# A 4096-cubed matmul with gelu: the check reads A's first block later, and one summed unit of B is read from the input

## The chip, the cores and the metric

The kernel runs on one core of a Trainium2 chip. The metric is device time in microseconds (us), of which the median of the timed runs counts. The core has five instruction streams: TensorE (PE), VectorE (DVE), ScalarE (ACT), GpSimd (POOL) and SyncE (SP). In this kernel POOL only issues transfers into the core (and a few within DRAM), and SP only issues stores.

## The reference

```python
def reference(a, b):            # a: [4096, 4096] f32, b: [4096, 4096] f32
    x = np.matmul(a, b)
    return 0.5 * x * (1 + np.tanh(np.sqrt(2 / np.pi) * (x + 0.044715 * x**3)))
```

## The kernel before, in words

A and B are read as f32 and land as f16 (the transfer converts). The product is computed by a Strassen-like scheme with seven products P1 to P7 of half-size blocks: A and B each have quadrants "11", "12", "21", "22", and a product takes a sum of quadrants of A times a sum of quadrants of B. The output is cut into 16 groups (mb, nb): mb is one of four bands of rows, nb one of four bands of columns. A band's quadrant of B has two chunks along the inner dimension (`c` 0 and 1).

*Groups 0 to 3* ("raw groups", `first_group`, `raw_group`) are computed for mb = 0 while B is read for the first time. Sums of B's quadrants are made there on VectorE (`combine2`, L964) and stored in DRAM as summed units, one for each (nb, product name): `unit(nb, name)`, DRAM tile `k_unit`, four quarters of 512 KB, stored on SP by `store_unit`, fetched later on POOL by `fetch_unit_to`.

*The 12 other groups* run as six late pairs (`late_pair`, numbered 4, 6, 8, 10, 12, 14, about 170 us each, starting near 419, 590, 760, 931, 1101 and 1271 us). Pairs 4, 8 and 12 work on nb 3 and 0, pairs 6, 10 and 14 on nb 1 and 2. Each pair goes through the seven products (`both`), and for each obtains the two summed units of B by `whole_pair`. Some products need a plain quadrant of B and no sum: those named in `FROM_INPUT` are not stored by a raw group but read again from the input, as 16 pieces of 128 KB (8 for a chunk), until a pair named in `STORE_AT` has stored them:

```python
elif (nb, name) in FROM_INPUT and (nb, name) not in on_hand:
    ...
        dma("POOL", dst, src, [], toks, "raw_b", batch=("bl", nb, name, cc))
    ...
else:
    for q in (2 * cc, 2 * cc + 1):
        fetch_unit_to(nb, name, q, cells[q])
```

*The first group* (mb = 0, nb = 0) starts when nothing is in the core. It opens with chunk 0 of A11 times that of B12 (`first_steps`, which issue eight A loads and eight B loads of 128 KB ahead of all others), then `plain_pe` (L2260) takes plain quadrants, A11 times B11 first and, four products later, the one with B21 (each of 32 matmuls); then come the sums. `load_b_` and `load_a_` issue the loads: B's pieces are 128 KB, A's 256 KB. A arrives with its rows in the wrong dimension, so VectorE transposes each chunk (L656). Half-products (L744) follow, with sums of A and B from L964, and their results are copied on ScalarE (L1316, L2384) and added on VectorE (L1322).

*The check.* In f16 the result holds only for inputs of moderate size. The kernel therefore sums squares of A's rows and of B's columns (`stats["a"]`, `stats["b"]`), and a last test decides whether a general path has to run instead; in the runs here it does not. For A's first band ScalarE squares each 128x256 piece while it lies there (`weigh_row`, L684: an ACTIVATE with an accumulator, and the instruction that reads the accumulator). Later bands of A are squared in the pairs. For B the squares of nb = 0 are taken in the first group, by VectorE (L1405) or by ScalarE (L1408) as the table `SQ` says, and are added up on VectorE (L1413).

*Order.* All but the first steps is written down as operations with a number (class `Plan`), and a planner sorts them by costs and due times (`MOVE`, `WEIGHT`, `COST`). Its order is then corrected by tables of numbers: `EARLIER` moves an operation's due time, `AFTER` puts operation n behind m on its engine, `HOLD` makes one wait for another. PE's order is fixed. Each engine runs its stream in that order, so a POOL load that waits for its buffer holds the loads behind it. Names such as `bR_79`, `stage_87`, `aD_82` and `aT` are buffers in the core; a 128x2048 f16 cell is 512 KB, and a chunk is two cells.

Of the kernel before, what the change touches and what calls it, by code (L numbers as in the profile page):

```python
# [9 lines left out]
F16 = mybir.dt.float16  # L10
# [8 lines left out]
Q = 32  # L19
# [33 lines left out]
UNDER_WAY = {"POOL": [(0.68, 12.2)] * 4}  # L53
# [7 lines left out]
    "store": 1.345, "fetch": 1.38, "quarter": 1.6, "piece": 1.27, "out": 0.73, "raw_a": 1.3, "raw_b": 0.645,  # L61
    "raw_a0": 1.363, "raw_b0": 0.64, "tiny": 0.2, "out_half": 0.3,
}
WEIGHT = {
    "raw_a0": 1.31, "raw_b0": 1.06, "store": 2.0, "fetch": 2.42, "quarter": 2.16, "piece": 2.16, "raw_a": 1.11,
    "raw_b": 1.06, "out": 1.05,
# [15 lines left out]
def modes_of(**kw):  # L82
# [12 lines left out]
}  # L95
HOLD = {
   
}
AFTER = [
# [459 lines left out]
def half_path(  # L559
# [281 lines left out]
    def c(x):  # L841
        return ("c", x)
# [1681 lines left out]
```

## Time and profile before

| what | us |
|---|---|
| median of 3 runs | 1445.19 |
| fastest and slowest of them | 1443.98, 1448.59 |
| the profiled execution | 1448.0 |
| its span in the trace | 1446.4 |
| mean granted clock of PE | 0.999 |

The profile is of one execution. In rows of the trace the first number is the start in us from the span's start, the second the length; in brackets stands how long the engine was idle before it, and what released it. A row of the waits has the engine and line that waited, what it waited for, the sum in us, the count and the longest. A row of a window has the length, for each engine its busy time and instructions (PE, PEld, DVE, ACT, POOL), the granted clock of PE, the share of the transfer engines and GB/s. A row of the transfers has their count, size and the median us from issue to landing.

### The profile page before, as it was taken

The numbers are of one execution on the slowest core, as the hardware profiler recorded it, in microseconds if no ns is written. First come the engines' busy times: TensorE is split into PE (matmuls) and PEld (weight loads), VectorE is DVE, ScalarE is ACT, GpSimd is POOL, SyncE is SP. The second block draws the span as 40 slices with busy tenths as digits, with TensorE's granted clock in tenths as the row PEclk, the third lists the DMA queues.
The fourth block names the chain that finished last, engine by engine and source line by source line (L and its number), as shares of the span: only waits on it lengthen the run. The fifth ranks groups of instructions, "written<-read, shape, count | busy, mean of one in ns | idle before, by whom it ended". The sixth has DMA issues, their size and how long they took to land. (4 is left out here: it accounts for less than half of the span.)

```text
span 1446.4 us, 19351 instructions
## 1 busy us (share of the span) xinstructions
PE 1419.4 (98%) x6707; PEld 656.3 (45%) x6707; DVE 1238.0 (86%) x1331; ACT 692.1 (48%) x1492; POOL 487.5 (34%) x892
## 2 busy tenths in 40 slices
PE   8989999999999999999999999999999999999998
PEld 3434455465444444444444444444444444444443
DVE  2997797998889999979897988887998998878876
ACT  4966656358866313543655313353463622333133
POOL 6554245054225152324423342332322231231220
PEclk9999999999999999999999999999999999999999
DMA  9999999999999998989979897998998967796773
GB/s 171 203 241 272 311 298 266 338 237 271 295 299 248 335 201 231 310 276 276 321 259 318 274 216 270 257 248 276 280 348 241 302 160 228 273 313 217 260 256 140
DMA packets 207674, 380.99 MB, mean 263 GB/s; under 512 B 20944, under 2 KB 119760, under 8 KB 207568
## 3 DMA queue, kind: packets, MB, share of 16 engines
q0 software_dynamic: 150400, 247.52, 71.7%
q1 hardware_dynamic: 57168, 132.15, 24.4%
q8 instruction: 55, 0.90, 0.2%
q14 instruction: 51, 0.42, 0.1%
HBM read 339.74 MB, written 134.22 MB: 328 GB/s over the span
## 5 line engine op out<-in xcount | busy, mean ns | idle before, releaser
L1972 PE MATMUL acc<-bR 128*128 128x512 f16 x1568 | 346.8, 379 | 0.4 <-DVE bR L964 0.2
L1972 PEld LDWEIGHTS <-bR 128*128 128x128 f16 x1984 | 193.9, 98 | 235.0 <-DVE bR L964 1.3
L1972 PE MATMUL acc<-bR,aT 128*128 128x512 f16 x1280 | 283.4, 379 | 4.8 <-DVE bR L964 3.9
L1972 PEld LDWEIGHTS <-aT 128*128 128x128 f16 x1664 | 162.6, 98 | 202.0 <-issue 6.2
L838 POOL DMA_DIRECT2D bR<-k_unit x224 | 121.4, 545 | 367.9 <-PE acc L1972 265.2
L964 DVE TENSOR_TENSOR bR<-bR 128x4096 f16<-128x4096 f16 (+1 forms) x114 | 210.6, 1858 | 29.6 <-PE acc L1972 20.3
L838 POOL DMA_DIRECT2D bR<-in_b_dram x320 | 173.6, 546 | 159.0 <-DMA bR<-in_b_dram 61.3
L1984 ACT COPY acc<-acc 128x512 f32<-128x512 f32 x168 | 95.7, 574 | 274.7 <-PE acc L1972 247.4
L1322 DVE TENSOR_TENSOR y<-acc,y 128x512 f32<-128x512 f32 x269 | 177.1, 685 | 25.1 <-PE acc L1972 24.2
L1972 PE MATMUL acc<-bR,aD 128*128 128x512 f16 x736 | 163.6, 379 | 0.0
L1296 ACT ACTIVATE y<-y 128x512 f32<-128x512 f32 x174 | 105.3, 625 | 112.2 <-DVE y L1322 111.9
L1972 PEld LDWEIGHTS <-aD 128*128 128x128 f16 x1024 | 100.2, 98 | 120.8
L744 PE MATMUL acc<-bR,aT 128*128 128x512 f16 x544 | 119.9, 379 | 2.2 <-DVE y L1322 1.2
L744 PEld LDWEIGHTS <-aT 128*128 128x128 f16 x768 | 75.1, 98 | 92.3 <-issue 3.3
L1981 ACT COPY y<-acc 128x512 f32<-128x512 f32 x114 | 66.4, 585 | 94.5 <-PE acc L1972 87.1
L1408 ACT ACTIVATE y<-bR 128x1024 bf16<-128x1024 f16 x83 | 84.9, 1051 | 36.5 <-DVE y L1413 33.8
L838 POOL DMA_DIRECT2D stage<-in_b_dram x104 | 56.3, 546 | 121.9 <-PE acc L1045 32.3
L744 PEld LDWEIGHTS <-aD 128*128 128x128 f16 x608 | 59.4, 98 | 77.9 <-DVE aD L964 4.2
L1972 PE MATMUL acc<-stage,bR 128*128 128x512 f16 x416 | 94.0, 379 | 0.0
L1413 DVE TENSOR_TENSOR y<-y 128x1024 bf16<-128x1024 bf16 x102 | 70.0, 688 | 25.6 <-ACT y L1408 24.0
L1972 PE MATMUL acc<-stage,aT 128*128 128x512 f16 x384 | 86.8, 379 | 0.0
L1327 DVE TENSOR_TENSOR acc<-acc,y 128x512 f32<-128x512 f32 x115 | 78.9, 693 | 5.3 <-ACT y L1981 5.0
(128 smaller groups left out, 1769.0 us busy)
## 6 DMA issues: line engine op xcount, KB each, us to landing
bR<-k_unit POOLq DMA_DIRECT2D x224, 512.0 KB, 7.8
out_dram<-y SPq DMA_DIRECT2D x194, 256.0 KB, 6.8
bR<-in_b_dram POOLq DMA_DIRECT2D x328, 128.0 KB, 7.0
k_unit<-bR SPq DMA_DIRECT2D x78, 512.0 KB, 7.0
stage<-k_unit POOLq DMA_DIRECT2D x60, 512.0 KB, 7.0
bR<-in_a_dram POOLq DMA_DIRECT2D x64, 256.0 KB, 9.2
k_unit<-stage SPq DMA_DIRECT2D x30, 512.0 KB, 8.0
out_dram<-bR SPq DMA_DIRECT2D x56, 256.0 KB, 6.7
```

Of the source, the lines that this page charges most:

```text
L744: nc.tensor.matmul(acc, sa[:, j // 2, i * P : (i + 1) * P, j % 2], sb[:, j, :], start=start and j == 0, stop=stop and j == 3, skip_group_c ...
L838: return plan.add(queue, COST[queue], lambda: eng.dma_start(out=dst, in_=src), r=r, w=w, size=MOVE[what] * SPREAD, weight=weight, **kw)
L964: nc.vector.tensor_tensor(out=dst, in0=xa, in1=ya, op=ALU.add if op > 0 else ALU.subtract)
L1296: act("gelu", lambda: nc.scalar.activation(t, t, ACT.Gelu_apprx_tanh), [("f", f)], [("f", f)])
L1322: dve("add", lambda: nc.vector.tensor_tensor(out=sm(g), in0=bank(s, i), in1=sm(f), op=ALU.add), [("f", f)], [("f", g), ("p", s, i)])
L1327: dve("add", lambda: nc.vector.tensor_tensor(out=bank(s, i), in0=bank(s, i), in1=sm(f), op=ALU.add), [("f", f)], [("p", s, i)])
L1408: act("square", lambda t=t, src=src: nc.scalar.activation(t, src, ACT.Square), [c(cx)], [("f", f)], slack=60.0, lead=lead)
L1413: dve("add16", lambda t=t, u=u: nc.vector.tensor_tensor(out=u, in0=u, in1=t, op=ALU.add), [("f", f)], [("f", e)], slack=60.0, lead=lead)
L1972: nc.tensor.matmul(bank(w, i), sa[:, jx // 2, r * P : (r + 1) * P, jx % 2], bv[:, jx, :], start=p in "17" and jx == 0, stop=jx == NJ - 1, ...
L1981: act("copy", lambda: nc.scalar.copy(out=sm(f), in_=bank(w, i)), [("p", w, i)], [("f", f)])
L1984: act("copy", lambda: nc.scalar.copy(out=bank(*dst), in_=bank(*x)), [("p", *x)], [("p", *dst)])
```

## The change

1. *A's first band is squared later.* The 128 squares on ScalarE in the first group go, with the two small VectorE steps that added them up. In pairs 8 and 12 the four quadrants of that band are read again from the input: eight times a chunk (`new_chunk`), each by four POOL loads of 256 KB (32 in all), followed by eight ScalarE squares of 128x512 (64 in all); the chunk is then free again. `AGAIN` says before which product of the pair each one is placed.
2. *The unit (1, P1)* enters `FROM_INPUT`. Its raw group no longer stores it (four SP stores of 512 KB less there). Pairs 6, 10 and 14 take it from the input (48 POOL loads of 128 KB instead of 12 fetches of 512 KB). `STORE_AT` has 14 for it, so pair 14 stores it (four SP stores), after which nothing fetches it.
3. *Squares of B for nb = 0*: `SQ` is False throughout, so 12 squares of 128x1024 go from VectorE to ScalarE.
4. *Order.* B11's chunk 0 gets a lead of 500 over A21's, and the tables `MOVE`, `WEIGHT`, `EARLIER`, `HOLD` and `AFTER` are new.

PE's instructions are the same in number and order of work.

```diff
-SQ = {"12": True, "11": True, "22": False, "21": True}
+SQ = {'12': False, '11': False, '22': False, '21': False}
-FROM_INPUT = ((0, 'P1'), (0, 'P2'), (0, 'P3'), (1, 'P2'), (1, 'P3'), (3, 'P3'))
-STORE_AT = {(0, 'P1'): 4, (0, 'P2'): 4, (1, 'P2'): 14, (0, 'P3'): 8}
+FROM_INPUT = ((0, 'P1'), (0, 'P2'), (0, 'P3'), (1, 'P2'), (1, 'P3'), (3, 'P3'), (1, 'P1'))
+STORE_AT = {(0, 'P1'): 4, (0, 'P2'): 4, (1, 'P2'): 14, (0, 'P3'): 8, (1, 'P1'): 14}
+AGAIN = {8: {'P6': ('11', 0), 'P5': ('11', 1), 'P3': ('12', 0), 'P4': ('12', 1)}, 12: {'P6': ('21', 0), 'P5': ('21', 1), 'P3': ('22', 0), 'P4': ('22', 1)}}
+AGAIN_SLACK = 20.0
+LEAD11 = 500.0
-        load_b_("11", 0)
+        load_b_("11", 0, LEAD11)
...
-HOLD = {
-   
+    1268: 1267, 2046: 2154, 3152: 3249,
...
+    def weigh_again(quad, h, x0):
+        ih, kh = int(quad[0]) - 1, int(quad[1]) - 1
+        n = NX // 2
+        s, toks, t = chunk(x0).rearrange("p (x r) -> p x r", r=CH * RUN), [c(x0), c(x0 + 1)], rows_again[ih]
+        gate = [o for o in plan.ops if o.eng == "PE"][-CAST_BACK:][:1]
+        for g in range(4):
+            dma("POOL", s[g * Q : (g + 1) * Q, :, :], a_v[kh, g, :, ih * MH // Q + h * n : ih * MH // Q + (h + 1) * n, :],
+                [], toks, "raw_a", batch=("again", quad, h), slack=AGAIN_SLACK, after=gate)
+        for x in range(n):
+            r = h * n + x
+            act("weigh", lambda x=x, r=r: nc.scalar.activation(
+                s[:, x, :], s[:, x, :], ACT.Square, accum_out=t[:, kh, r : r + 1]),
+                [], [("again", ih), *toks], batch=("wa", quad, h), slack=SLACK)
+        if kh and h:
+            dve("small", lambda: nc.vector.tensor_reduce(
...
+            if name in again:
+                x = new_chunk()
+                weigh_again(*again.pop(name), x)
+                free_cells.extend((x, x + 1))
...
-            for r in range(NX):
-                act("weigh0", lambda r=r: weigh_first(quad, cc, (r,), next(junk)), toks,
-                    [("w0",), ("rows", 0), ("rows", 1)],
-                    batch=("w0", quad, cc), slack=FIRST_SLACK)
...
-        dve("stat", weigh_first_half, [("w0",)], [("sa", 0, 0), ("sa", 0, 1)], slack=300.0)
```

What moves on POOL, at three places. First the loads right behind the first steps: `bR_79` takes B11, chunk 0, and `stage_87` A21, chunk 0. Before:

```order
L838 DMA bR_79<-in_b_dram 32x4x512 x5
L838 DMA stage_87<-in_a_dram 32x16x256
L838 DMA bR_79<-in_b_dram 32x4x512 x3
L838 DMA stage_87<-in_a_dram 32x16x256
L838 DMA bR_75<-in_b_dram 32x4x512
```

After:

```order
L897 DMA bR_79<-in_b_dram 32x4x512 x8
L897 DMA stage_87<-in_a_dram 32x16x256 x4
L897 DMA bR_75<-in_b_dram 32x4x512
L897 DMA bR_80<-in_b_dram 32x4x512
L897 DMA bR_75<-in_b_dram 32x4x512
```

A21's loads now begin only when all eight pieces of B11 are issued.

Next, the loads up to the last piece of `bR_77`, which takes B21, chunk 0 (`bR_75`, `bR_74` and `bR_80` take other quadrants of B, `stage` and `aD` quadrants of A). The rows before follow directly on those of the place above; after, one row lies between (`stage_86`, two loads of A). Before:

```order
L838 DMA stage_86<-in_a_dram 32x16x256
L838 DMA stage_87<-in_a_dram 32x16x256 x2
L838 DMA stage_86<-in_a_dram 32x16x256 x2
L838 DMA bR_77<-in_b_dram 32x4x512 x2
L838 DMA stage_86<-in_a_dram 32x16x256
L838 DMA bR_77<-in_b_dram 32x4x512 x2
L838 DMA bR_75<-in_b_dram 32x4x512 x3
L838 DMA aD_82<-in_a_dram 32x16x256 x2
L838 DMA bR_75<-in_b_dram 32x4x512 x4
L838 DMA aD_82<-in_a_dram 32x16x256 x2
L838 DMA stage_87<-in_a_dram 32x16x256 x4
L838 DMA bR_77<-in_b_dram 32x4x512 x4
```

After:

```order
L897 DMA bR_75<-in_b_dram 32x4x512 x2
L897 DMA bR_74<-in_b_dram 32x4x512
L897 DMA stage_86<-in_a_dram 32x16x256 x2
L897 DMA bR_80<-in_b_dram 32x4x512
L897 DMA bR_74<-in_b_dram 32x4x512
L897 DMA bR_77<-in_b_dram 32x4x512
L897 DMA bR_75<-in_b_dram 32x4x512 x4
L897 DMA bR_80<-in_b_dram 32x4x512
L897 DMA bR_77<-in_b_dram 32x4x512 x6
L897 DMA bR_80<-in_b_dram 32x4x512
L897 DMA aD_82<-in_a_dram 32x16x256 x2
L897 DMA bR_77<-in_b_dram 32x4x512
```

Fewer pieces of A stand ahead of the last piece of `bR_77` now, and more of B.

Last, in pair 8, the loads of `stage_87` with eight raw pieces of B (chunk 1 of the unit for the next sum). Before:

```order
L838 DMA bR_77<-in_b_dram 32x4x512
L838 DMA bR_74<-in_b_dram 32x4x512
L838 DMA stage_86<-in_b_dram 32x4x512
L838 DMA bR_77<-in_b_dram 32x4x512 x5
L838 DMA bR_74<-in_b_dram 32x4x512 x3
L838 DMA stage_87<-in_b_dram 32x4x512 x8
L838 DMA bR_77<-in_b_dram 32x4x512
L838 DMA bR_75<-k_unit_233 128x2048
```

After:

```order
L897 DMA bR_74<-in_b_dram 32x4x512 x4
L897 DMA bR_73<-in_b_dram 32x4x512 x8
L897 DMA bR_74<-in_b_dram 32x4x512 x4
L897 DMA bR_75<-in_b_dram 32x4x512
L897 DMA bR_76<-in_a_dram 32x8x512
L897 DMA stage_87<-in_b_dram 32x4x512 x8
L897 DMA bR_76<-in_a_dram 32x8x512
L897 DMA bR_75<-in_b_dram 32x4x512 x7
L897 DMA bR_76<-in_a_dram 32x8x512
L897 DMA k_unit_240<-in_b_dram 32x4x512
L897 DMA bR_76<-in_a_dram 32x8x512
```

One of the four A loads of a second reading (`bR_76`) now stands directly ahead of the eight pieces of `stage_87`, the three others among those behind it.

More of the change, by code (lines that the diff above doesn't have):

```diff
@@ L1 @@
 from contextlib import ExitStack
-from itertools import cycle
 import concourse.bass as bass
@@ L52 @@
 BUSY = {"PE": 20.2, "DVE": 15.3, "ACT": 20.4, "POOL": 12.2, "SP": 5.0}
-UNDER_WAY = {"POOL": [(0.68, 12.2)] * 4}
+UNDER_WAY = {"POOL": [(0.68, 13.2)] * 4}
 LAG = 0.2
@@ L60 @@
 MOVE = {
-    "store": 1.345, "fetch": 1.38, "quarter": 1.6, "piece": 1.27, "out": 0.73, "raw_a": 1.3, "raw_b": 0.645,
-    "raw_a0": 1.363, "raw_b0": 0.64, "tiny": 0.2, "out_half": 0.3,
+    "store": 1.31, "fetch": 1.291, "quarter": 1.6, "piece": 1.27, "out": 0.743, "raw_a": 1.304, "raw_b": 0.649,
+    "raw_a0": 1.377, "raw_b0": 0.6444, "tiny": 0.2, "out_half": 0.3,
 }
 WEIGHT = {
-    "raw_a0": 1.31, "raw_b0": 1.06, "store": 2.0, "fetch": 2.42, "quarter": 2.16, "piece": 2.16, "raw_a": 1.11,
-    "raw_b": 1.06, "out": 1.05,
+    "raw_a0": 1.263, "raw_b0": 1.13, "store": 2.06, "fetch": 2.18, "quarter": 2.16, "piece": 2.16, "raw_a": 1.22,
+    "raw_b": 0.98, "out": 1.14,
 }
@@ L680, in load @@
             nc.gpsimd.dma_start(out=dst, in_=src)
-    def weigh_row(dst, src, to=None):
-        nc.scalar.activation(src if to is None else to, src, ACT.Square, accum_out=dst)
-    def weigh_first(quad, c, xs, to=None):
-        ih, kh = int(quad[0]) - 1, int(quad[1]) - 1
-        for x in xs:
-            k = ((kh * CH + c) * 2 + ih) * NX + x
-            weigh_row(stats["a"][:, k : k + 1], staged[quad, c][:, x, :], None if to is None else to[:, :])
-    def weigh_first_half():
-        t = tallies[:, 4 * NX : 6 * NX]
-        nc.vector.tensor_reduce(
-            out=t, in_=stats["a"].rearrange("p (k x) -> p x k", k=2 * CH), axis=AX.X, op=ALU.add
-        )
-        nc.vector.tensor_copy(out=stats["a"][:, : 2 * NX], in_=t)
     def gather(s):
@@ L792, in half_path @@
     before = {}
-    for n, whats in ((0, "A11_0a B12_0a A11_0b B12_0b T11_0a T11_0r T11_0s W11_0"),):
+    for n, whats in ((0, "A11_0a B12_0a A11_0b B12_0b T11_0a T11_0r T11_0s"),):
         for what in whats.split():
             half = what[-1] == "0" and what != "A11_0"
-            if what[0] == "W":
-                before.setdefault(n, []).append((weigh_first, (what[1:3], int(what[4]), range(NX))))
-                continue
             for h in (0, 1) if half else (None,):
@@ L1331, in half_path @@
     next_stage = [0]
-    rows = [tallies[:, 2 * ih * NX : 2 * (ih + 1) * NX].rearrange("p (k x) -> p k x", k=2) for ih in range(2)]
+    rows, rows_again = (
+        [tallies[:, 2 * k * NX : 2 * (k + 1) * NX].rearrange("p (k x) -> p k x", k=2) for k in (2 * n, 2 * n + 1)]
+        for n in range(2)
+    )
     seen_rows = set()
@@ L1369, in turn_quad @@
         seen_rows.add((mb, ih))
+    def weigh_again(quad, h, x0):
[13 more added lines that the diff above has]
+            dve("small", lambda: nc.vector.tensor_reduce(
+                out=stats["a"][:, ih * NX : (ih + 1) * NX], in_=t.rearrange("p k x -> p x k"), axis=AX.X, op=ALU.add,
+            ), [("again", ih)], [("sa", 0, ih)], slack=60.0)
     def load_raw(nb, quad, slot):
@@ L1432, in fn @@
                 )
-            dve("stat", fn, [("f", e), ("w0",)], [("f", f), ("sb", k)], slack=60.0)
+            dve("stat", fn, [("f", e)], [("f", f), ("sb", k)], slack=60.0)
     SB, SA, ST = (18, 19, 20, 21), (22, 23, 16, 17), (12, 13, 14, 15)
@@ L2058, in split_pair @@
                 then()
+        again = dict(AGAIN.get(ga, {}))
         def both(name, fresh, done):
+            if name in again:
+                x = new_chunk()
+                weigh_again(*again.pop(name), x)
+                free_cells.extend((x, x + 1))
             for what in CASTS.get((ga, name), ()):
@@ L2227, in first_group @@
         X, Y = 0, 1
-        junk = cycle((stats["b"].bitcast(F16), tallies.bitcast(F16)))
         S = {quad: slot_cells(b_slot[quad]) for quad in b_slot}
```

400 rows, old and new, of tables (AFTER, EARLIER) are left out of this document.

## The prediction

> **What bounds the kernel now.** I read the page's first part, then PE's waits, then PE's rows with idle time before them, then the DMA list of two stretches.
>
> ```profile
> PE 1419.4 (98%) x6707; PEld 656.3 (45%) x6707; DVE 1238.0 (86%) x1331; ACT 692.1 (48%) x1492; POOL 487.5 (34%) x892
> ```
>
> PE is busy 98% of 1446.4 us, so an edit that leaves the matmuls alone can only move PE's waits and its clock. The waits of the profiled execution, without the two of the start-up, are:
>
> ```profile
> PE acc L2260 <- DMA bR<-in_b_dram: 4.5, 3, 2.9
> PE acc L744 <- DVE aD L964: 4.4, 3, 1.9
> PE acc L1972 <- DVE bR L964: 4.1, 3, 2.4
> PE acc L744 <- DVE stage L964: 2.1, 2, 1.8
> PE acc L744 <- DVE y L1322: 1.2, 1, 1.2
> PE acc L744 <- ACT acc L2384: 1.0, 1, 1.0
> PE acc L1972 <- DMA bR<-in_b_dram: 0.8, 1, 0.8
> PE acc L1972 <- DMA bR<-k_unit: 0.2, 1, 0.2
> ```
>
> They sum to 18.3 us: the whole prize, beside the clock. Where they lie, by PE's rows (start, length, work, idle before it):
>
> ```profile
> 23.20 29.32 PE L2260 MATMUL acc<-bR,aT 128*128 128x512 f16 x128 [2.88 <-DMA bR<-in_b_dram]
> 53.15 0.38 PE L2260 MATMUL acc<-bR,aT 128*128 128x512 f16 x1 [0.63 <-DMA bR<-in_b_dram]
> 54.48 20.66 PE L2260 MATMUL acc<-bR,aT 128*128 128x512 f16 x95 [0.95 <-DMA bR<-in_b_dram]
> ...
> 94.38 3.63 PE L744 MATMUL acc<-bR,aD 128*128 128x512 f16 x16 [1.87 <-DVE aD L964]
> 115.70 7.07 PE L744 MATMUL acc<-aD,aT 128*128 128x512 f16 x32 [1.17 <-DVE aD L964]
> ...
> 180.32 7.07 PE L744 MATMUL acc<-stage,aD 128*128 128x512 f16 x32 [1.85 <-DVE stage L964]
> ...
> 448.55 3.61 PE L1972 MATMUL acc<-bR,aT 128*128 128x512 f16 x16 [1.48 <-DVE bR L964]
> 863.99 7.08 PE L1972 MATMUL acc<-bR,aT 128*128 128x512 f16 x32 [2.38 <-DVE bR L964]
> ```
>
> Three groups: the start to 116 us (4.5 + 4.4 + 1.0 = 9.9), the raw groups to 284 us (2.1 + 1.2 = 3.3), the late pairs (4.1 + 0.8 + 0.2 = 5.1). No row after 863.99 has an idle time: the last 577 us have nothing to win, only to lose.
>
> **The start: the order of the loads.** In the first 60 us POOL's loads run at the rate that the transfers allow.
>
> ```profile
> 23.20:26.61 3.41, 3.41 (x9) 1.26 (x9) 0.00 (x0) 0.00 (x0) 1.93 (x4) 0.54 1.41 197
> 26.61:30.02 3.41, 3.41 (x18) 1.57 (x16) 0.01 (x1) 0.03 (x1) 1.09 (x2) 1.00 1.45 196
> 31.49 0.54 POOL L838 DMA_DIRECT2D bR<-in_b_dram  x1 [0.77 <-DMA stage<-in_a_dram]
> 32.83 0.54 POOL L838 DMA_DIRECT2D bR<-in_b_dram  x1 [0.80 <-DMA stage<-in_a_dram]
> ```
>
> The windows' last column is GB/s: 196 to 197. POOL's issues stand 1.34 us apart there, waiting for A loads; an A load is 256 KB, 262 kB at 196 GB/s, 1.34 us too. So bytes ahead in the queue give the landing time.
>
> *B11, chunk 0.* Before, one A load lies within its last eight pieces, now none: it lands 1.34 us earlier, 2.88 becomes 1.54. *B21, chunk 0.* Counted in both orders up to its last piece, A has 8 of 128 KB and 16 of 256 KB before, 8 and 10 now; B has 32 and 38 pieces of 128 KB: 9216 KB before, 8448 KB now. 768 KB less is 786 kB, at 197 GB/s 4.0 us. It lands near 50.4 instead of 54.4, and PE, 1.34 us earlier, wants it at 51.2: 0.63 and 0.95 go. Together 2.9 us. Bounds 0 (another piece is late) and 4.5 (all three go).
>
> Then VectorE and ScalarE. ScalarE's rows to 130 us, VectorE's squares, POOL's hold, and the stretch 60 to 126:
>
> ```profile
> L684 ACT ACTIVATE stat_b<-stage 128x256 f16<-128x256 f16 x40 | 16.4, 409 | 9.1 <-DMA stage<-in_a_dram 9.1
> L684 ACT ACTIVATION_READ_ACCUMULATOR stat_b<-stage 128x1 f32 x40 | 7.7, 193 | 0.0
> L1408 ACT ACTIVATE bR<-bR 128x1024 bf16<-128x1024 f16 x9 | 9.2, 1048 | 7.9 <-DVE y L1413 5.2 <-DMA bR<-in_b_dram 2.7
> L1405 DVE TENSOR_TENSOR bR<-bR x9: 650/683/687, 32.9 to 71.8; 128x1024 bf16<-128x1024 f16 x9
> 88.32 4.28 POOL L838 DMA_DIRECT2D stage<-in_b_dram x8 [7.83 <-ACT tally L684]
> 60.00:126.00 66.00, 60.58 (x279) 26.98 (x277) 61.39 (x79) 43.89 (x144) 33.81 (x62) 1.00 1.21 242
> ```
>
> A row square costs ScalarE 0.409 + 0.193 = 0.60 us; 128 of them are 77 us, all before 116. They go, and 12 squares of B come from VectorE, 12 x 1.05 = 12.6 us: ScalarE has room, and POOL's hold of 7.83 us behind it goes. VectorE loses 12 x 0.68 = 8.2 us before 72 us. It is busy 61.39 of the 66 us in which PE waits 4.4 + 1.0 for its sums and for a ScalarE copy, so less backlog there shortens waits. But the second chunk of A21 is now loaded last of the first block: its transposes and sum come later, and I expect a new wait of 0.8 to 2 us near 81 us, where before has none. I take 5.4 down to 2.1: gain 3.3. Bounds: 5.4 (all go) and a loss of 0.5 (all stay, B21's gain merely waits elsewhere, plus a little). Start: 2.9 + 3.3 = 6.2 us, bounds -0.5 to 9.9.
>
> The clock after a wait, in three windows of one length:
>
> ```profile
> 863.99:867.40 3.41, 3.41 (x16) 1.56 (x16) 3.41 (x5) 1.08 (x2) 0.00 (x0) 1.00 0.97 359
> 94.38:97.80 3.42, 3.42 (x16) 1.58 (x17) 3.42 (x6) 0.00 (x0) 2.34 (x5) 1.00 1.22 198
> ```
>
> Behind the waits of 2.38 and 1.87 us the granted clock is 1.00; behind that of 2.88 it was 0.54 (23.20 to 26.61 above: 9 matmuls, 18 in the next window). That half cost 3.41 / 2 = 1.7 us. With a wait of 1.54 it may not come, but I count nothing: PE would reach B21 at 49.5 and wait there for 50.4, and the late sum of A21 stands behind it. By the Trainium skill, "TensorE: Matmul & The Clock Gate", section "What's actually happening", the half rate comes after a whole idle window of about 3.4 us; here 2.88 us sufficed, so the trace is stricter. By that rule a shorter wait would surely not halve the clock, and at most 0.8 us more would be left at B21.
>
> **The raw groups.** Four 512 KB stores of the unit (1, P1) go from SP's queue. 2.1 MB at the 303 GB/s below is 6.9 us of transfers. The wait at 180.32 is for a sum of late B pieces, which shared the wires with such stores; the whole stretch now starts earlier, so part of the room is eaten. I take a quarter of 3.3: 0.8. Bounds 3.3 and -1 (the B pieces also moved).
>
> **The pairs: what is added.** Rows of 126 to 283 us first, then of pair 8 (760 to 931 us):
>
> ```profile
> DMA packets 26391, 47.60 MB, mean 303 GB/s; under 512 B 2932, under 2 KB 15894, under 8 KB 26380
> bR<-in_b_dram POOLq DMA_DIRECT2D x82, 128.0 KB, 9.0
> stage<-in_b_dram POOLq DMA_DIRECT2D x16, 128.0 KB, 7.2
> ...
> DMA packets 22502, 44.62 MB, mean 261 GB/s; under 512 B 2284, under 2 KB 12268, under 8 KB 22490
> k_unit<-in_b_dram POOLq DMA_DIRECT2D x16, 128.0 KB, 7.3
> stage<-in_b_dram POOLq DMA_DIRECT2D x16, 128.0 KB, 6.6
> bR<-in_b_dram POOLq DMA_DIRECT2D x16, 128.0 KB, 5.3
> bR<-in_a_dram POOLq DMA_DIRECT2D x6, 256.0 KB, 11.7
> stage<-in_a_dram POOLq DMA_DIRECT2D x4, 256.0 KB, 8.3
> ```
>
> Pairs 8 and 12 each read 16 A pieces again (16 x 1.34 = 21 us of transfers, 16 issues) and square them: 32 squares, by width at most 1.05 + 0.19 us each, 40 us of a ScalarE that is 48% busy over a pair of 171 us. Hidden. A raw piece is read as f32 and lands as f16, so counts twice in memory: the raw groups carried 47.60 + 98 x 0.131 = 60.4 MB in 157 us, 385 GB/s, with 3.3 us of waits. Pair 8 carries 44.62 + 48 x 0.131 + 10 x 0.262 = 53.5 MB, and 8.4 more: 62 MB in 171 us, 362 GB/s. That is under what the raw groups bore. Pairs 6, 10 and 14 load (1, P1) as 16 raw pieces instead of four 512 KB units each: as many landed bytes, twice the reading, twelve issues more, on a POOL that is 34% busy. The words of the change say the unit is stored at its first reuse; its entry says 14, and the order has no fetch of it left: all three uses read the input.
>
> The order in pair 8 keeps the stall before 863.99:
>
> ```profile
> 826.95 0.56 POOL L838 DMA_DIRECT2D stage<-in_b_dram  x1 [15.35 <-DVE bR L964]
> 850.41 4.87 POOL L838 DMA_DIRECT2D stage<-in_b_dram  x8 [0.65 <-DMA bR<-in_b_dram]
> ```
>
> From the issue at 850.41 to PE at 863.99 are 13.6 us. Now, counted in PE's order, the buffer is freed 49 matmuls before its reader: 49 x 7.08/32 = 10.8 us, with an A piece just ahead. Stall 2.8 (1 to 5). Several other loads are released as close. I take the pairs' waits from 5.1 to 6.6: a loss of 1.5. Bounds: a gain of 5.1, and a loss of 7 (pairs 8 and 12 each lose what the raw groups lose, 3.5 us).
>
> **Sum.** -6.2 - 0.8 + 1.5 = -5.5 us. The profiled execution took 1448.0 us, 2.8 above the median 1445.2; 5.5 off the median is 1439.7.
>
> **Rivals.**
> *B, given back:* the gain is made by 126 us, but pairs 6 and 8 wait for it again: they run at the transfers' pace, and a PE that comes 6 us earlier finds loads released as late as before. For it: the pieces at 863.99 are 13.6 us in flight. Against it: loads there are released by PE and VectorE, which move along. Loss of 5 instead of 1.5: 1443.2.
> *C, slower:* each of the eight second readings holds a chunk and puts 4 x 1.34 = 5.4 us of transfers in front of the fetch behind it. Where a buffer is freed under 13.6 us before its reader, that adds to the stall. It decides once over 6.9 us are lost: two of eight such places at 5.4 are 10.8, so 1445.2 - 7.0 + 10.8 = 1449; three give 1454. Against: after 863.99 PE has no wait at all before, so pair 12 has slack to give.
> By the Trainium skill, "DMA: Bandwidth & Descriptors", section "Specifications", one core gets about 358 GB/s of memory; by it pair 8's 62 MB would need 173 us, 2 more than it has, and the sum would be 1441.7. The 385 GB/s of the raw groups is over that figure, so the trace speaks against it.
> *D, more:* the early waits nearly all go (9.9) and the pairs lose nothing: 1445.2 - 9.9 - 0.8 = 1434.5.
>
> **How the numbers follow.** My forecast 0.47 (its own range 1437 to 1442), B 0.25, C 0.15, D 0.13. The range reaches to D and to where C begins: 1434 to 1448. About 0.3% (4.3 us) is what a measurement of this kernel can tell from no change: faster is under 1440.9, slower over 1449.5. Faster 0.40 of mine and D: 0.53; same 0.07 and B: 0.32; slower 0.15.
>
> **What would show it.** In the profile after: the wait of 2.88 near 1.5 and no wait for B21; POOL no longer held by ScalarE; a new wait for A21's sum near 80 us; the matmul group at 115.70 starting near 109.5; no more than 7 us of waits after 419 us, one of them in pair 8 for a VectorE sum of stage pieces. I am wrong if group 115.70 starts after 113, or if a fetch behind a second reading of A stops PE.

## The result, and the profile after

| | before | after |
|---|---|---|
| median of the runs, us | 1445.03 (8 runs) | 1453.72 (8 runs, 1450.40 to 1461.48) |
| profiled execution, us | 1448.0 | 1451.07 |

The ratio is 1.0063, with a 95% interval of 1.0039 to 1.0086: slower by 8.7 us. The two profiled executions differ by 3.1 us only: that of before lies 3 us above its median, that of after 2.7 below its own. So the rows below show part of the loss, and single executions are read here only for waits that come back in several kernels. Of all executions reported in this document one, of the twelve of b_p1_not_stored, took 2521.79 us at a mean granted clock of 0.556; it is left out of that kernel's numbers.

PE's line of the page, then all that PE waited for in the execution after, down to 1.0 us (sum, count, longest):

```profile
PE 1421.8 (98%) x6707; PEld 656.0 (45%) x6707; DVE 1227.5 (85%) x1319; ACT 688.1 (47%) x1376; POOL 526.5 (36%) x960
```

```profile
PE acc L806 <- DVE aD L1023: 3.7, 1, 3.7
PE acc L2052 <- DMA bR<-in_b_dram: 2.7, 4, 1.5
PE acc L2052 <- DMA bR<-k_unit: 2.3, 3, 1.2
PE acc L2052 <- DVE bR L1023: 2.1, 2, 1.2
PE acc L806 <- DVE stage L1023: 1.5, 2, 1.1
PE acc L2052 <- ACT y L2061: 1.5, 2, 1.2
...
PE acc L2341 <- DMA bR<-in_b_dram: 1.4, 1, 1.4
PE acc L806 <- DMA stage<-in_b_dram: 1.3, 1, 1.3
...
PE acc L2052 <- ACT bR L1375: 1.0, 1, 1.0
```

Line 2052 is the matmul of the late pairs, 1972 before. Its waits are 9.6 us now (2.7 + 2.3 + 2.1 + 1.5 + 1.0), 5.1 before. PE's rows with idle time, from the start and from the pairs:

```profile
21.95 6.85 PE L2341 MATMUL acc<-bR,aT 128*128 128x512 f16 x31 [1.39 <-DMA bR<-in_b_dram]
...
82.31 8.67 PE L806 MATMUL acc<-aD 128*128 128x512 f16 x32 [3.68 <-DVE aD L1023]
111.71 7.07 PE L806 MATMUL acc<-aD,aT 128*128 128x512 f16 x32
322.76 3.40 PE L806 MATMUL acc<-stage,aT 128*128 128x512 f16 x15 [1.28 <-DMA stage<-in_b_dram]
444.99 3.61 PE L2052 MATMUL acc<-bR,aT 128*128 128x512 f16 x16 [0.91 <-DVE bR L1023]
546.81 3.61 PE L2052 MATMUL acc<-bR,aD 128*128 128x512 f16 x16 [1.52 <-DMA bR<-in_b_dram]
620.81 3.61 PE L2052 MATMUL acc<-bR,aT 128*128 128x512 f16 x16 [1.03 <-ACT bR L1375]
850.33 3.61 PE L2052 MATMUL acc<-bR 128*128 128x512 f16 x16 [1.16 <-ACT y L2061]
960.95 3.63 PE L2052 MATMUL acc<-bR,aD 128*128 128x512 f16 x16 [1.23 <-DMA bR<-k_unit]
...
1440.27 3.62 PE L2052 MATMUL acc<-bR,aT 128*128 128x512 f16 x16
```

The group at 111.71 is the one that started at 115.70, the group at 444.99 the one at 448.55. The last group starts at 1440.27, and before at 1437.25:

```profile
1437.25 3.62 PE L1972 MATMUL acc<-bR,aT 128*128 128x512 f16 x16
```

So 4.0 us were won at the start, 3.6 were left at the first pair, and the pairs turned them into 3.0 us lost: 6.6 us in the pairs. In between, the group of 283.90 starts at 277.94, 6.0 earlier: the raw groups win 2.0 us up to there and lose 2.4 behind it.

The gain at the start is smaller than these rows make it. The profiled execution of before is late there itself: in the five kernels below that keep before's order up to 116 us (b_p1_raw, b_p1_stored_at_6, b_p1_not_stored, b_p1_cast, b_pairs_of_after) the group of 115.70 starts between 114.01 and 114.62. Against these, after wins 2.3 to 2.9 us.

### The profile page after: what moved, and what is told of

Read it like the earlier page. It is cut to its first block, busy times and chain, and to the rows that moved or that the text cites. A ratio compares the mean times of both kernels' runs of the same rounds, so it can differ in the third digit from the quotient of the medians.

```text
span 1449.5 us, 19215 instructions
## 1 busy us (share of the span) xinstructions
PE 1421.8 (98%) x6707; PEld 656.0 (45%) x6707; DVE 1227.5 (85%) x1319; ACT 688.1 (47%) x1376; POOL 526.5 (36%) x960
## 4 chain that ended last, share of the span: by engine, by line
PE 76%; DMA 14%; POOL 4%; DVE 3%; issue 2%; ACT 1%; DVEq 0%; SPq 0%; POOLq 0%; ACTq 0%
PE acc L2052 61%; PE acc L806 13%; DMA bR<-in_b_dram 5%; DMA bR<-k_unit 3%; POOL bR L897 2%; DMA stage<-in_a_dram 2%; PE acc L1104 2%; DMA stage<-in_b_dram 2%; DVE bR L1023 1%; DMA bR<-in_a_dram 1%; DMA aD<-in_a_dram 1%; DMA out_dram<-bR 1%; POOL stage L897 1%; DVE y L1381 0%; DVE aD L1023 0%
## 5 line engine op out<-in xcount | busy, mean ns | idle before, releaser
L2052 PE MATMUL acc<-bR 128*128 128x512 f16 x1344 | 298.4, 379 | 1.5 <-ACT y L2061 1.5
L897 POOL DMA_DIRECT2D bR<-in_b_dram x384 | 208.1, 545 | 210.5 <-PE acc L2052 46.4
L2052 PEld LDWEIGHTS <-bR 128*128 128x128 f16 x1824 | 178.4, 98 | 217.1 <-issue 2.0
L897 POOL DMA_DIRECT2D bR<-k_unit x198 | 107.8, 547 | 318.1 <-PE acc L2052 140.7
L1023 DVE TENSOR_TENSOR bR<-bR 128x4096 f16<-128x4096 f16 (+1 forms) x107 | 195.3, 1830 | 28.8 <-PE acc L2052 18.2
L2052 PE MATMUL acc<-bR,aD 128*128 128x512 f16 x752 | 168.2, 379 | 4.7 <-DMA bR<-in_b_dram 2.3
L1488 ACT ACTIVATE y<-bR 128x1024 bf16<-128x1024 f16 x86 | 88.4, 1052 | 45.7 <-DVE y L1493 41.0
L2052 PE MATMUL acc<-stage,bR 128*128 128x512 f16 x480 | 108.0, 379 | 0.0
L897 POOL DMA_DIRECT2D bR<-in_a_dram x108 | 63.1, 588 | 100.8 <-ACT bR L1421 37.2
```

Of the source, the lines that this page charges most:

```text
L897: return plan.add(queue, COST[queue], lambda: eng.dma_start(out=dst, in_=src), r=r, w=w, size=MOVE[what] * SPREAD, weight=weight, **kw)
L1023: nc.vector.tensor_tensor(out=dst, in0=xa, in1=ya, op=ALU.add if op > 0 else ALU.subtract)
L1488: act("square", lambda t=t, src=src: nc.scalar.activation(t, src, ACT.Square), [c(cx)], [("f", f)], slack=60.0, lead=lead)
L2052: nc.tensor.matmul(bank(w, i), sa[:, jx // 2, r * P : (r + 1) * P, jx % 2], bv[:, jx, :], start=p in "17" and jx == 0, stop=jx == NJ - 1, ...
```

## The experiments

All were timed beside the kernel before on the same chip, in five rounds; the chip differs between some of the experiments, so kernels are compared by their ratios to before. Where a kernel's names begin with a, it is made from the kernel after, with b from the kernel before.

**Is it the second reading of A?** Loads and squares out:

```diff
-            dma("POOL", s[...], a_v[...], [], toks, "raw_a", batch=("again", quad, h), slack=AGAIN_SLACK, after=gate)
+            o = dma(...); o.fn = lambda: None      # nothing is issued, the order stays
```

> The kernel after, with the 32 second loads of A's first band and their 64 squares left out (its sum for the check is set to 0), all else in the same order. Theory R (the second reading is what the pairs lost: its loads, its squares and the chunks that they hold): the pairs' part, from the matmul at 445 us to the end, comes back to about the length of before, so some 6 us less than after: about 1447. Theory O (the order: PE comes some 4 us earlier into pairs whose loads are released as late as before, by new tables): within 2 us of after, 1452 to 1455.

Both kernels without the squares (this and the next) ended in the kernel's general path, which it takes where the sum of the squares is not as it should be, and here it was 0: 5317 and 5318 us in all. Only their first 1450 us can be read. There the pairs lost as in after: the waits of the product that starts at 546.81 (1.52 in after) are 2.01 and 2.60.

> The kernel after, with the second loads of A kept and only their 64 squares left out. If the second reading costs by its transfers, this equals after (1453 to 1455). If it costs because loads in POOL's queue wait for ScalarE's squares to give the chunk back (50.8 us of such waits in the profile after), this equals the kernel without both, about 1447 by theory R. By theory O both stay near 1453.

So the first was run again with a sum that keeps it out of that path.

> The kernel after without the 32 second loads and 64 squares, as in the first such run, with the sum set to 1024, so that the general path is not taken and the total can be read. By the waits of that first run (8 us lost between 445 and 968 us although nothing is read again) the total stays near after's: 1451 to 1455. Theory R would have 1447.

Measured: 1455.25 us, ratio 1.0066 (1.0043 to 1.0090), as after. The second reading costs nothing that can be measured, although POOL now waits for its squares: in the profile after

```profile
POOL bR L897 <- ACT bR L1443: 50.8, 6, 13.6
```

six loads wait 50.8 us for a chunk that ScalarE has not yet given back (L1443 is the square of the second reading). Taking this away did not lower the total. Theory R, which had 1447, falls.

**Is it the raw pieces of (1, P1)?** First in after's order:

> The kernel after, where pairs 6, 10 and 14 get the unit (1, P1) by four fetches of 512 KB (of another stored unit of the same shape, so the values are not those of the product) instead of 16 raw pieces; the four stores in pair 14 are left out. If the raw pieces cost (theory P): pairs 6 and 10 lose the waits at 621 and 939 to 965 us, about 3 us less: 1450. By theories R and O: 1452 to 1455.

Measured: 1452.43, 1.0052 (1.0032 to 1.0073). Not told apart from after. Then in before's order, raw in all three pairs, and raw in pair 6 alone:

```diff
-                        fetch_unit_to(nb, name, q, cells[q])       # pairs 6, 10, 14
+                        ... q odd: the chunk's eight pieces from the input; q even: nothing
```

> The kernel before with only the unit (1, P1) changed: not stored in its raw group, and read as 16 raw pieces in pairs 6, 10 and 14 at the places of its fetches; all else in before's order. If raw pieces instead of units cost (theory P): 2 to 4 us more, 1447 to 1449. If not: 1444 to 1446.

> The kernel before, with the unit (1, P1) not stored in its raw group but read as 16 raw pieces in pair 6, stored there (four stores 12 us behind the loads) and fetched as a unit in pairs 10 and 14. In the kernel that read it raw three times the raw groups gained 5.5 us and the pairs lost 19. If the loss is the raw pieces in 10 and 14, this keeps most of the gain: 1441 to 1445. If any raw reading delays what stands behind it, pair 6 alone costs 3 us and more: 1445 to 1449.

Measured: 1459.57, 1.0101 (1.0081 to 1.0120), and 1451.69, 1.0050 (1.0034 to 1.0066). Both are above what was expected (1449 at most), so in before's order raw pieces cost plainly, and more than theory P had. A row of PE in pair 10 of the first kernel and one in pair 6 of the second:

```profile
934.84 8.28 PE L1978 MATMUL acc<-bR,aT 128*128 128x512 f16 x31 [4.98 <-DMA bR<-in_b_dram]
```

```profile
600.37 4.72 PE L1991 MATMUL acc<-bR,aT 128*128 128x512 f16 x15 [5.39 <-DMA bR<-in_b_dram]
```

Eight pieces that go where two fetches went come 5 us late. In after's order no pair waits more than 1.52 us for pieces of B; what that order costs elsewhere is the question of the next runs.

**What do the pieces of the early part give?** The squares alone, and POOL's order alone:

> The kernel before, with only the 128 squares of A's first band in the first group left out (their sum is set to 1024); same order otherwise. What the prediction took for the start would show here as far as it comes from ScalarE: POOL's hold of 7.83 us goes and the matmul group at 115.70 us starts 1 to 3 us earlier; the total is 1442 to 1445. If the squares were hidden, group 115.70 moves by less than 0.5 us and the total stays 1444 to 1446.

> The kernel before, with only POOL's order at the start changed: B11's eight pieces ahead of A21's first, and the last four pieces of B21 ahead of six loads of A. The waits of 2.88, 0.63 and 0.95 us become 1.5, 0 and 0: 2.9 us at the matmul that starts at 54.48. If the pairs keep a gain (no theory E), the total is 1441 to 1443; if the sums at 94 to 116 us eat it, 1444 to 1446.

Measured: 1445.97, 1.0003 (0.9990 to 1.0016), and 1446.17, 1.0000 (0.9984 to 1.0016). Neither gives anything. Without the squares POOL's hold goes, but the waits for VectorE's sums stay (4.4 before, 4.0 here), and the group of 115.70 starts at 114.60, as in the five kernels with before's start. In the second, the loads of B do come earlier, and PE is done with the 32 matmuls on B11 at 28.80, 3.0 us before it was:

```profile
21.73 7.07 PE L2261 MATMUL acc<-bR,aT 128*128 128x512 f16 x32 [1.59 <-DMA bR<-in_b_dram]
30.91 3.41 PE L2261 MATMUL acc<-bR,aT 128*128 128x512 f16 x15 [2.11 <-ACT stat_b L685]
```

The wait of 2.11 us is one for A21: the weight loads of these matmuls wait for VectorE's transpose of it, which waits for the load and ends at 30.86. (The row of the matmul names an accumulator read on ScalarE that ends at the same time; the matmuls do not read what it writes.)

```profile
30.91 2.06 PEld L2261 LDWEIGHTS <-aT 128*128 128x128 f16 x11 [2.60 <-DVE aT L657]
```

```profile
29.61 1.25 DVE L657 STREAM_TRANSPOSE aT<-stage 128x1024 uint32<-128x1024 uint32 x1 [14.38 <-DMA stage<-in_a_dram]
```

Then come a wait of 0.48 for a copy on ScalarE, one of 1.57 for an add on VectorE and one of 2.40 for a sum, and at the group of 94.38 nothing is left (94.56). In after, where A21's first four loads stand together behind B11's eight, the transpose begins at 27.98 and the wait is 0.47. So B11's gain needs A21 in time as well; whether it also needs the squares out of the way, no run shows. The stores of (1, P1), alone:

> The kernel before with the four stores of (1, P1) left out and its three uses served by fetches of another stored unit (so the values are not those of the product): the price of the stores alone, in before's order. By the two runs that left these stores out, 5 us of waits go between 107 and 284 us. If the pairs keep it: 1440 to 1442; if they take it back: 1444 to 1447.

Measured: 1441.25, 0.9976 (0.9965 to 0.9987), beside 1446.13 on this chip: about 4 us (3.5 by the ratio, 4.9 by the medians). This is the part of the change that gains. From 107 us to the first pair one wait is left, and the last group starts at 1429.52 where before has it at 1437.25:

```profile
107.18 7.08 PE L744 MATMUL acc<-bR,aD 128*128 128x512 f16 x32 [1.33 <-DVE aD L964]
```

```profile
1429.52 3.62 PE L1974 MATMUL acc<-bR,aT 128*128 128x512 f16 x16
```

**Do the pairs take back whatever comes early?** A trial to win the 3.68 us at 82 us:

> The kernel after, with the eight loads of A21 and A22, chunk 1, moved ahead of ten pieces of B in POOL's queue; nothing else changes. If the wait of 3.68 us at 82.3 us comes from these loads being late, it goes, with the half clock behind it (1.6 us): up to 5 us less at 116 us. If lateness at the start is what limits the total, the total follows: about 1449. If the pairs take every early gain back (theory O), the total stays at 1452 to 1455.

Measured: 1468.89, 1.0168 (1.0143 to 1.0193), 15 us worse than after. VectorE waited for the pieces of B that had been put behind, with the adds that PE needed queued behind that wait:

```profile
77.90 1.22 DVE L1024 TENSOR_TENSOR aD<-bR 128x2048 f16<-128x2048 f16 x1 [13.19 <-DMA bR<-in_b_dram]
```

```profile
79.78 3.57 PE L2342 MATMUL acc<-bR,aT 128*128 128x512 f16 x8 [10.96 <-DVE y L1382]
```

It answers the question all the same. PE reaches the group of 444.99 at 456.36, 7.8 us after before, and that of 960.95 at 979.65, 19.0 after before (960.69 there): these pairs lose 11 us even for a PE that comes late. The opposite case:

> The kernel before, with everything up to the first pair in after's order, B's squares of the first group on ScalarE, and A's first-band squares left out (their sum for the check is set to 4096). The unit (1, P1) is stored and fetched as before, and the six pairs have before's order word for word. Theory O (the pairs' new order makes their loads late): the early gain of 3 to 5 us at 445 us stays, total 1439 to 1442. Theory E (a PE that comes earlier into the pairs waits there whatever the order): it is given back, 1444 to 1446.

Its total (5279 us) again holds the general path, so the expected totals are not tested. With the stores back, after's order of the start and the raw groups has waits of 5.42 us at 159.42 and 7.79 at 375.39, both for sums on VectorE, and PE was 14.7 us late at the first pair and 14.2 late at 892 us. So the early PE that this run was to test did not come about. What tests theory E is b_p1_not_stored: its PE comes 5.8 us early into before's order of the pairs (442.73) and is 7.7 early at the end. Before's order loses nothing, early or late. Theory E falls.

**The order itself.** Two approximate exchanges:

> The kernel before with its own work (no second reading of A, (1, P1) stored and fetched) and its own start, but the operations of the six pairs brought as near to after's order as their buffers allow. Theory O: the pairs lose about 6 us as in after: about 1451. Theory E and theory R (the second reading): nothing is lost, 1444 to 1446.

> The kernel after with all its work and its own start, but the operations of the six pairs as near to before's order as their buffers allow; the second loads of A and the raw pieces of (1, P1) stand where the dependences and after's times put them. Theory O: the pairs lose only what the added work costs, total 1443 to 1448. Theory R: as after, 1452 to 1455.

Measured: 1459.12, 1.0093 (1.0069 to 1.0117), and 1529.40, 1.0593 (1.0559 to 1.0627). The first loses as theory O has it, but 8 us more than it said; its order is only near to after's, so this is no measure of it. The second missed by 80 us; we read this as added loads pushed into an order without room for them, and it says nothing on what after's own order costs. The clean test leaves after's order word for word and takes both added loads out:

> The kernel after with neither of its added loads: no second reading of A (sum set to 1024) and (1, P1) by fetches of 512 KB of another stored unit, so that its six pairs move as many bytes as before's, in after's order word for word. Theory O (the order alone makes the pairs lose): still 1450 to 1455. Theory W (the added loads together, where either alone could be removed without effect): 1441 to 1446.

Measured: 1450.26, 1.0035 (1.0019 to 1.0051). It moves the same bytes as b_p1_not_stored, has 128 squares less (1.0003 without them in before's order) and takes 8.5 us longer by the two ratios. What differs beyond that is the order, with 12 squares of B on ScalarE, which no run separates. Where, by the starts of the same groups in the two profiles:

| group, start before | a_no_added_loads | b_p1_not_stored | difference |
|---|---|---|---|
| 115.70 | 111.39 | 114.10 | -2.7 |
| 283.90 | 278.09 | 278.48 | -0.4 |
| 448.55 | 445.63 | 442.73 | 2.9 |
| 1437.25 | 1439.41 | 1429.52 | 9.9 |

The new order wins 2.7 us up to 112 us, loses 5.6 until the first pair and 7.0 in the pairs; of these 7.0, 1.7 are a half clock behind a wait of 2.35 us at 710.47. The added loads together come to 1.0063 against 1.0035, about 4 us, with intervals that overlap.

Then two of its tight places were put back as before has them:

```diff
 AFTER = [ ...
+    (1983, 1910), (1981, 1983), (2910, 2890),
 ]
```

> The kernel after with two places of the pairs' order put back as before has them: in pair 4 two fetches of 512 KB go behind the last raw piece of the product at matmul 2595 (546.81 us, wait 1.52, in the other runs of this order 1.7 to 3.3), and in pair 8 one copy of a bank on ScalarE goes ahead of another (850.33 us, wait 1.16 in every run of this order). Theory O: both waits go, and the total falls by 2 to 4 us, 1450 to 1452, if nothing behind takes them up; if the pairs lose by the sum of transfers, the waits come back at the next load and the total stays at 1453 to 1455.

Measured: 1451.98, 1.0041 (1.0023 to 1.0058). Both waits are gone:

```profile
544.80 5.34 PE L2053 MATMUL acc<-bR,aD 128*128 128x512 f16 x24
549.99 2.32 PE L2053 MATMUL acc<-bR 128*128 128x512 f16 x10
...
849.94 3.62 PE L2053 MATMUL acc<-bR 128*128 128x512 f16 x16
853.39 3.62 PE L2053 MATMUL acc<-stage,aT 128*128 128x512 f16 x16
```

By the ratios the total is 3.2 us under after's, where 2 to 4 were expected; the intervals overlap. In the profile half of the two waits comes back at other loads (0.97 us at 839.57): from the group of 444.99 to the last one it takes 993.9 us, after 995.3. That these two places waited because of their order is shown by their rows; what they are worth in the total is not. For the other places of the pairs it was not tried.

**A version that beats both.** Keep before's order, drop the stores, and make the unit where POOL has nothing to do:

```diff
+CAST_AT = [466.0] * 8 + [541.0] * 8
...
+            nc.gpsimd.dma_start(out=<piece of unit(1, "P1")>, in_=<piece of b>)     # within DRAM, 16 times
```

> A version made from the runs so far, complete: the kernel before, where the raw group does not store (1, P1), and 16 transfers of 128 KB within DRAM make the unit from the input in pair 4 instead, eight at 466 us and eight at 541 us, where POOL waited 12 and 13 us with nothing to issue; all three uses fetch it as before. The stores alone are worth 4 us (0.9976 in the run without them). If the casts hide in pair 4: 1441 to 1443. If their 10.7 us of transfers make pair 4 wait: 1444 to 1448. By theory E it would be 1446 whatever happens.

Measured: 1443.44 beside 1447.18 before, 0.9971 (0.9959 to 0.9983): 3.7 us faster, about the whole worth of the stores. The casts need no buffer in the core. POOL issues them in two stretches in which it waited before (470.87 to 481.94 and 544.46 to 554.03), and the loads behind them are issued at 483.61 and 558.88, before at 483.25 and 557.98. The profiled execution is the slowest of the six, with a wait of 3.21 us at 369.38, ahead of the pairs; from the group of 448.55 to the last it takes 988.2 us, before 988.7.

## Why the prediction was wrong

*What held.* B11's wait became 1.39 (1.54 was said), B21's 0.63 and 0.95 went: the group of 54.48 started at 50.22, 4.3 us earlier, where the loads were given 2.9. The squares read again are hidden. POOL is no longer held by ScalarE at the start. The group of 115.70 started at 111.71 (109.5 said, wrong from 113).

*The half clock* went with the shorter wait and came back later:

```profile
82.31:85.72 3.41, 3.41 (x9) 1.28 (x10) 3.41 (x4) 0.00 (x0) 1.18 (x3) 0.52 1.38 186
85.72:89.13 3.41, 3.41 (x18) 1.51 (x17) 3.41 (x5) 0.00 (x0) 0.00 (x0) 1.00 1.35 205
```

Behind the 3.68 us it is 0.52 for one window, 9 matmuls instead of 18. The wait for A21's sum was foreseen as 0.8 to 2 us; it was 3.68, and that alone covers the 2.2 us that are missing between 6.2 us for the start and the 4.0 measured (2.3 to 2.9 against the five kernels with before's start). The half clock added little at 111.71: in a_no_added_loads a wait of 3.64 us at the same place left the clock at 1.00, but PE then waits 0.70, 0.22 and 0.20 us behind it and reaches the group at 111.39. So what failed at the start is the gain of 3.3 us from VectorE and ScalarE: up to 54 us the loads had won 4.3, at 111.71 no more than 4.0 is left. A21 also isn't the last load, as was said (four loads of A follow at 79.25); its second chunk stands behind ten pieces of B that stood behind it before.

*The step that failed* is the term of the pairs, and with it the order, which the sum put at nothing. The pairs were given a loss of 1.5 us, argued from one stall (2.8 said, 1.17 measured), with "several other loads are released as close" beside it; they lost 6.6 in the profile. The prediction priced what was added (loads, squares, bytes) and not that the order of some 2600 instructions outside PE was laid anew there, and that of the raw groups too. The runs put about 8 us on that order, in the raw groups and in the pairs, with the same work and the same bytes, and some 4, not well resolved, on the added loads. With the 4 us that the stores gain, this makes the 8.7 measured. Which places of the order cost it stays open but for the two that were tried.

*The stores of (1, P1)* were taken for 0.8 us, a quarter of the raw groups' waits. Alone they are worth about 4. ScalarE's relief, on which the start's 3.3 us rested in part, is worth nothing alone; VectorE's was in no run alone.

*Rivals.* Rival B had the right place and too small a size: 5 us where 6.6 were lost in the profile and more in the median; but its reason, that an early PE meets loads as late as before, is refuted by b_p1_not_stored and b_p1_cast. Rival C named the second reading, and a_no_reread_2 refutes it; that its sign was right and its 1454 lies beside the 1453.72 measured is luck. The range ended at 1448, where rival C began; the bound of the pairs beside it, a loss of 7, took the raw groups' waits for the pairs, a figure for transfers and not for an order.

## What to carry to other kernels

Where an order written by hand or by a planner is replaced over a long stretch without waits, that replacement is an edit with a price of its own, and before it is run nothing bounds it but the slack of each load; give it a wide term. Test each edit in the old order by making operations empty or exchanging them in place: so a 4 us gain was found inside a change that lost 9. Count, for each load, the time from the release of its buffer to its reader, and look first where it is under the 13.6 us that one took from issue to PE. This is a place to look and no price: the load in pair 8, counted at 10.8 us, made PE wait 1.17 and not 2.8.

## What the runs showed of the hardware

16 transfers of 128 KB within DRAM, issued where the queue was idle, cost nothing that can be measured (0.9971 with them, 0.9976 without making the unit at all), where 16 pieces into buffers in the core, at one place, made PE wait 5.39 us and gave 1.0050.

The length of a wait does not settle whether PE's clock halves. The wait of 3.68 us in after halved it; one of 3.68 us in a_two_places, at the same work, did not; and one of 2.05 us in a_no_reread did (783.68, 0.58 behind it), where 2.38 before did not. In the traces the clock changes on a fixed grid of 3.41 us, and what goes with it is how much of the window before PE was busy. After has one window with none:

```profile
78.74:82.15 3.41, 0.00 (x0) 0.00 (x0) 3.41 (x4) 0.00 (x0) 2.98 (x6) 1.00 1.23 195
82.15:85.56 3.41, 3.25 (x8) 1.20 (x9) 3.41 (x5) 0.00 (x0) 1.34 (x3) 0.50 1.38 186
```

In a_two_places the wait falls across two windows, each 46% busy, and the clock stays:

```profile
78.21:81.63 3.42, 1.56 (x8) 0.49 (x5) 3.42 (x5) 0.00 (x0) 2.32 (x4) 1.00 1.24 201
81.63:85.04 3.41, 1.58 (x8) 0.76 (x9) 3.41 (x5) 0.00 (x0) 2.95 (x6) 1.00 1.24 170
```

Counted over all traces up to 1435 us, each of the 34 full-clock windows with PE under 43% busy is followed by one at half clock, and of the others one, at 44%.

One kernel's executions spread over 11 us (after, 1450.40 to 1461.48). The two with a mean clock of 0.999 took 1450.40 and 1451.77, the three with 0.996 took 1454.88 to 1461.48, so part of the loss may lie in halved windows that the one profile does not have; it hides two thirds of the 8.7 us.
